# A hybrid recurrence and MoE layer on one core: the last eight gate projections move ahead of the gated-delta steps

## The chip, the cores and the metric

The kernel runs on 1 core of one Trainium2 chip. Times are device microseconds (us) of one execution, as the chip measures them. The profile and its trace come from one more execution, whose own time is given beside its span.

## What is computed

One layer over 256 latent tokens with a 256-token context, width 1024, all in f32: a projection, two bidirectional recurrences (gated delta and RWKV-7) that run first over the context and then over the latent tokens, a gated merge, and a mixture of 32 experts.

```
  u  = RMSNorm(h) * (1 + scale1) + shift1
  p  = u @ W_in                                  # also the columns of both gates gA, gB
  yA = GatedDeltaNet(p[A cols])                  # 4 + 4 chunks of 64, both directions
  yB = RWKV7(p[B cols])                          # bidirectional, column-major grid order
  h += gate1 * W_out( sig(p[gA]) * yA @ W_oA + sig(p[gB]) * yB @ W_oB )
  h += gate2 * HierMoE( RMSNorm(h) * (1 + scale2) + shift2 )

def step(s, inp):                                # one chunk of the gated delta rule
    v_new = u_c - w_c @ s
    o_c = qd_c @ s + qk_c @ v_new
    s = s * ge_c + kd_c.T @ v_new
```

The modulation rows (gate1, shift2, scale2, gate2) are products of silu(c) with the columns 2048 to 6143 of ada_w. They and the gates read only u and c, so neither depends on a recurrence.

## The kernel before, in words

Python writes the operations in program order and a scheduler orders each engine's instructions by their dependencies, by the buffers that they take in rings, and by priorities. The order of the middle of the program is a string, NB['go']; each letter calls one part (L1605), and some letters carry a priority (NB['hi']; G and r have none):

```
for x in NB["go"]:
    with hi(x):
        parts[x]()
TG, gm = t[2], n["G"]
...
k.rwkv_g()
...
k.gate_cols(range(max(gm, NB["g1"]), 16), ("pj", "ch", "ch"))
```

- **G** (filler, L1590) is one gate tile through gate_cols (L1052): a projection of 128 columns (proj, L350: 8 matmuls 128x256, which the trace shows as 16 records `pj<-u,w`, with two weight loads of 256 KB), a tanh on ACT, and a store to gscr. After each odd tile ada_rest (L253) makes one of eight modulation products: 8 matmuls 32x512, 16 records `ada<-w,silc`, with eight loads of 256 KB. Behind the last tile of each half ada_rows stores the sums.
- **r** is one of four latent RWKV-7 steps (rwkv_step; names rps, akps, ups, yps, sps). **R** is the same for the context. K, g, k, i, I, J, q, Q, V prepare the gated delta rule.
- gdn_step (L970) is one of eight gated-delta steps (0 to 3 context, 4 to 7 latent): it loads keys gkc and values gvc from scratch memory, transposes them (gkt, gvt), then gks (keys by state gS), gr on DVE, gup (by the triangular inverse TG), guu on ACT, gsp (state update), gS on DVE; a latent step also has gop, 16 pairs of small matmuls that give its output yo. gdn_post (L1039) ends the branch: a square on ACT, gon, Ln and Exp on ACT with a table load between them, two products on DVE.
- rwkv_post normalizes the RWKV-7 output (mean, then gate<-bg, yc). merge_b (L1083) multiplies it by w_o (`pab<-yc,w`), merge_a (L1093) does so for the gated-delta output (`pab<-post,w`), out_rows (L1100) multiplies by w_out into acc, and moe_quad (L1277) handles groups of four experts, whose weights wgu and wd (per expert 1024 x 512 and 256 x 1024 in f32) are streamed from HBM on SP's queue into six and seven slots.

Weight tiles of proj, ada_rest, merge and out_rows share a ring of 10 buffers of 256 KB (wraw, L340, pool "w"). From L1623 on a second pool "w2" of 12 buffers takes its place until the merge of the gated-delta branch. PSUM is divided in tags (L97): pj is one buffer of 512 columns, gc two, ch two. Gate tiles in filler use pj alone (NB['gt']). rwkv_g (L433) makes projection tile 30 with the tags EARLY (pj, gc, gc) and stands in program order behind the loop. gdn_step's gks, gup, gsp and gop use gc; gkt and gvt use pp.

Of the kernel before, what the change touches and what calls it, by code (L numbers as in the profile page):

```python
# [99 lines left out]
class K:  # L100
    def __init__(self, ctx, tc, A, dbg=None):
        self.nw = NB["w"]
        self.ctx, self.tc, self.nc, self.A, self.dbg = ctx, tc, tc.nc, A, dbg or {}
# [55 lines left out]
    def e(self, name, *dims, rows=P):  # L159
        return self.t(self.pe, name, *dims, tag="e", bufs=NB["e"], w=520, rows=rows)  # L160

    def rt(self, name, *dims):
        return self.t(self.prt, name, *dims, tag="rt", bufs=NB["rt"], w=520)

# [65 lines left out]
    def ada_first(self, hf, pool):  # L230
        ps = self.psum(NB["at"][0], name="ada0")[:, 0:512]

        for k in range(KD):
            w = self.t(pool, "aw", 2, 512, bufs=16)
            self.nc.sync.dma_start(w, self.A["ada_w"][k * P:(k + 1) * P, 0:2 * D]
                                   .rearrange("p (v c) -> p v c", v=2)[:, :, hf * 512:(hf + 1) * 512])
            for v in range(2):
                g = 2 * (k % 2) + v
                self.mm(ps[32 * g:32 * g + 32, :], self.sc[:, k, :], w[:, v, :], start=k < 2, stop=k > 5)
        a = self.e("a0", 512)  # L240
        self.nc.vector.tensor_copy(a, ps)
        pt = self.psum(NB["at"][1], name="adat")
        for j in range(4):
            self.lastada = self.mm(pt[:, j * 64:(j + 1) * 64], a[:, j * P:(j + 1) * P], self.cst("fold")).ins
        pv = pt[:, 0:256].rearrange("p (j v r) -> p v r j", j=4, v=2)[:, :, 0:2]
        m = self.mod[:, :, :, 4 * hf:4 * hf + 4]
        par = lambda n, v: self.parw(n).rearrange("p (v k) -> p v k", v=v)[:, :, 4 * hf:4 * hf + 4]
        for r in range(2):
            self.tt(m[:, :, r], pv[:, :, r], par("adab", 2), ALU.add)
            self.stt(m[:, 1, r], m[:, 1, r], 1.0, par("g1", 1)[:, 0], ALU.add, ALU.mult)  # L250


    def ada_rest(self, i, tags):  # L253
# [5 lines left out]
        if q == 0:  # L259
            self.copy(self.arow[b], ps, NB["aa"])  # L260
        else:
# [1158 lines left out]
EP0 = ((("wgu", 1), ("wd", 0)), (("wgu", 2), ("wd", 1)))  # L1420
EP1 = (("wgu", 3), ("wgu", 4), ("wd", 2))
PRE = (("wgu", 0), ("wgu", 1), ("wgu", 2), ("wd", 0), ("wgu", 3), ("wd", 1), ("wd", 2), ("wd", 3))
NB = {'st': 2, 'ys': 'PP', 'yc': [1, 1], 'hn': 'VAVA', 'im': 'AAPP', 'e': 7, 'rt': 13, 'w': 10, 'e1': 4, 'o2': 2, 'kvr': 2, 'cv': 'PVVPPVPPPVVV', 'g1': 3, 'g2': 0, 'imt': 1, 'gi': 0, 'hi': {'gp': 2000, 'R': 2000, 'i': 2000, 'gs': 2000, 'I': 2000, 'J': 2000, 'p11': 200, 'j0': 1500, 'g': 400, 'V': -400, 'rw': 2000}, 'zf': 1, 'g0': 1, 'pe': 0, 'vr': 'vr', 'jt': 'pp', 'go': 'KGGgGGRRGRRikIVGQqJrrrrG', 'rX': 1, 'rbk': 2, 'ixt': 1, 'vh': 2, 'bk': 4, 'ar': 3, 'gm': 7, 'fp': [[28, 'pj'], [29, 'gc'], [20, 'gc'], [21, 'ch'], [22, 'ch']], 'at': ['pp', 'sc'], 'pf': {'ma': 2, 'oo': 0.5}, 'pm': 8, 'aa': 1, 'gr': 0, 'gu': ['pj', 'gc', 'gc'], 'gq': 2, 'gk': 2, 'w2': 12, 'ip': [0, 0, 4], 'gt': ['pj']}


def layout(inp):
# [303 lines left out]
```

## Time and profile before

| | |
|---|---|
| median of 3 runs | 893.25 us (891.11 to 895.0) |
| the profiled execution | 896.1 us, its span 894.3 us |
| TensorE (PE) busy | 799.8 us, 89% of the span |
| VectorE (DVE), ScalarE (ACT), GpSimd (POOL) busy | 383.6, 229.2, 193.2 us |
| mean granted TensorE clock | 0.921 of full speed |
| HBM read, written | 189.64 MB, 19.94 MB |

Busy time is the time in which an engine executes. A granted clock of 1.00 is 2.4 GHz, of 0.5 is 1.2 GHz; a stretch between them had some time at each. "[0.63 <-DMA gkc<-kscr]" behind an instruction says that its engine was idle for 0.63 us before it and that the DMA into gkc ended the wait.

### The profile page before, as it was taken

The numbers are of one execution on the slowest core, as the hardware profiler recorded it, in microseconds if no ns is written. First come the engines' busy times: TensorE is split into PE (matmuls) and PEld (weight loads), VectorE is DVE, ScalarE is ACT, GpSimd is POOL, SyncE is SP. The second block draws the span as 40 slices with busy tenths as digits, with TensorE's granted clock in tenths as the row PEclk, the third lists the DMA queues.
The fourth block names the chain that finished last, engine by engine and source line by source line (L and its number), as shares of the span: only waits on it lengthen the run. The fifth ranks groups of instructions, "written<-read, shape, count | busy, mean of one in ns | idle before, by whom it ended". The sixth has DMA issues, their size and how long they took to land. (4 is left out here: it accounts for less than half of the span.)

```text
span 894.3 us, 15035 instructions
## 1 busy us (share of the span) xinstructions
PE 799.8 (89%) x6073; PEld 472.5 (53%) x6073; DVE 383.6 (43%) x799; ACT 229.2 (26%) x430; POOL 193.2 (22%) x279
## 2 busy tenths in 40 slices
PE   6999999898569999999899999999978996897785
PEld 1444567444246665767688776768444442332231
DVE  1322878999479446963235312133252210111012
ACT  0413465342363313344312231040030000000001
POOL 1012444336332626734211010000120000000000
PEclk9999999799668999997879988899999998998998
DMA  9722556323517762564641686666965999999993
GB/s 353 301 94 71 167 172 212 116 95 127 175 60 228 232 203 79 153 196 130 198 147 53 238 325 194 219 200 225 405 287 235 428 425 425 423 429 423 427 413 138
DMA packets 88359, 210.58 MB, mean 235 GB/s; under 512 B 7752, under 2 KB 37200, under 8 KB 80864
## 3 DMA queue, kind: packets, MB, share of 16 engines
q1 hardware_dynamic: 85248, 205.87, 62.9%
q10 hardware_dynamic: 3040, 3.74, 1.2%
q8 instruction: 48, 0.79, 0.4%
q14 instruction: 23, 0.19, 0.1%
HBM read 189.64 MB, written 19.94 MB: 234 GB/s over the span
## 5 line engine op out<-in xcount | busy, mean ns | idle before, releaser
L106 PE MATMUL pj<-u,w 128*128 128x256 f32 (+1 forms) x768 | 253.9, 483 | 2.5 <-ACT cxp L122 1.6
L106 PEld LDWEIGHTS pj<-u,w 128*128 128x128 f32 x768 | 146.2, 197 | 96.5 <-issue 75.6
L106 PE MATMUL gup<-wgu,xs 128*32 128x512 f32 x512 | 78.3, 678 | 22.1 <-DMA wgu<-in_wgu_dram 22.0
L106 PEld LDWEIGHTS gup<-wgu,xs 128*32 128x32 f32 x512 | 20.3, 122 | 76.1 <-issue 41.6
L112 DVE TENSOR_TENSOR msg<-msg,gup 128x256 f32<-128x256 f32 x8 | 3.4, 421 | 119.7 <-ACT msg L122 119.7
L112 POOL TENSOR_TENSOR rl<-rl,mhalf 128x1 f32<-128x1 f32 x2 | 1.1, 550 | 224.8 <-DVE rl L116 224.8
L112 DVE TENSOR_TENSOR itm<-ixt,imt 128x31 f32<-128x31 f32 (+22 forms) x89 | 40.1, 450 | 6.1 <-POOL ixt L546 4.1
L112 DVE TENSOR_TENSOR ixt<-ixt,itm 128x31 f32<-128x31 f32 (+22 forms) x89 | 41.6, 467 | 2.2
L106 PE MATMUL dnp<-wd,mhT 128*32 128x512 f32 x256 | 38.6, 598 | 4.1 <-DVE mhT L1326 4.1
L122 ACT ACT_TABLE_LOAD x24 | 30.8, 1283 | 22.4 <-PE ssq L106 10.4
L112 POOL TENSOR_TENSOR cacc<-cacc,cm 128x512 f32<-128x512 f32 (+1 forms) x24 | 26.5, 1106 | 43.1 <-ACT cm L122 31.6
L106 PEld LDWEIGHTS xsp<-oh,h 128*128 128x128 f32 x256 | 31.8, 199 | 6.2 <-issue 6.2
L106 PE MATMUL xsp<-oh,h 128*128 128x128 f32 x256 | 33.2, 283 | 0.0
L122 ACT ACTIVATE msg<-gup 128x256 f32<-128x256 f32 x8 | 3.1, 384 | 111.3 <-PE gup L106 111.3
L106 PE MATMUL acc<-my,ohT 128*128 128x512 f32 x64 | 29.7, 596 | 0.0
L106 PE MATMUL acc<-w,m 128*128 128x512 f32 x64 | 28.4, 594 | 0.6 <-DMA w<-in_w_out_dram 0.6
L112 POOL TENSOR_TENSOR gS<-gS,sdec 128x1024 f32<-128x1024 f32 x6 | 11.5, 1915 | 76.4 <-PE gop L106 45.2
L122 ACT ACTIVATE xs<-xsp 128x512 f32<-128x512 f32 x8 | 4.8, 597 | 90.4 <-PE xsp L106 90.4
L112 POOL TENSOR_TENSOR h<-xres,rowscale 128x512 f32<-128x512 f32 x4 | 5.1, 1270 | 105.1 <-DVE xres L112 105.1
L112 POOL TENSOR_TENSOR shs<-xp 128x512 f32<-128x512 f32 (+1 forms) x15 | 15.1, 1005 | 48.6 <-ACT xp L122 48.6
L106 PE MATMUL akps<-rA,rX 64*64 64x64 f32 x512 | 21.7, 241 | 2.8 <-ACT rtm L122 1.4
L106 PE MATMUL ada<-aw,silc 128*32 128x512 f32 x64 | 16.7, 716 | 8.2 <-DMA aw<-in_ada_w_dram 8.1
(371 smaller groups left out, 1305.3 us busy)
## 6 DMA issues: line engine op xcount, KB each, us to landing
wgu<-in_wgu_dram SPq DMA_DIRECT2D x28, 2048.0 KB
wd<-in_wd_dram SPq DMA_DIRECT2D x27, 1024.0 KB
w<-in_w_in_dram SPq DMA_DIRECT2D x96, 256.0 KB
w<-in_ada_w_dram SPq DMA_DIRECT2D x64, 256.0 KB
aw<-in_ada_w_dram SPq DMA_DIRECT2D x16, 512.0 KB
rX<-rscr SPq DMA_DIRECT2D x8, 768.0 KB
wgu<-in_wgu_dram SPq DMA_DIRECT2D x20, 256.0 KB
rscr<-bk SPq DMA_DIRECT2D x8, 512.0 KB
```

The lines of the kernel that those rows point to most:

```text
L106: return self.nc.tensor.matmul(out, lhsT, rhs, start=start, stop=stop)
L112: (eng or self.nc.vector).tensor_tensor(out=out, in0=a, in1=b, op=op)
L122: return self.nc.scalar.activation(out=out, in_=in_, func=func, **kw)
```

## The change

Eight more G stand at the end of the string, so the loop makes all sixteen gate tiles (tile 0 is made earlier, elsewhere), and with them the modulation products 4 to 7 and the second ada_rows. The call of gate_cols at L1625 then has an empty range. Nothing is added or removed: 8 projections, 8 tanh, 8 stores, 4 modulation products, and 48 loads (12.6 MB) are issued at another place in program order. They use the ring of pool "w" and the PSUM tag pj in place of "w2" and pj, ch, ch.

```
-'go': 'KGGgGGRRGRRikIVGQqJrrrrG'
+'go': 'KGGgGGRRGRRikIVGQqJrrrrGGGGGGGGG'
```

What the scheduler makes of it on PE is shown at two places; the rows are instructions in issue order, with the buffers' numbers only where a name needs one. The first is the start of the gated-delta chain, in the kernel before:

```order
L106 MATMUL rps<-ruv,rak 64x64 x8
L106 MATMUL rps<-sbd_1518,rA 64x128
L109 MATMUL gkt<-cs,gkc 128x128 x4
L106 MATMUL kqp<-gq,gk 64x64 x8
L106 MATMUL rps<-sbd_1518,rA 64x128 x4
L106 MATMUL gup<-gr_4602,TG 64x128 x8
L106 MATMUL rps<-sbd_1518,rA 64x128 x3
L106 MATMUL akps<-rA,rX 64x64 x18
L106 MATMUL gsp<-guu,gkd 128x128 x8
L106 MATMUL ups<-rr_3908,iT 64x64 x13
L106 MATMUL gks<-gS,gkc 64x128
L106 MATMUL ups<-rr_3908,iT 64x64 x3
```

The first gup and gsp (gr_4602 is that of step 0) stand among the matmuls of a latent RWKV-7 step. After the change, PE has these rows right behind the last `yps` of the last latent step:

```order
L106 MATMUL pj<-u,w 128x256 x8
L106 MATMUL mean<-yo,cs 128x512 x2
L106 MATMUL pj<-u,w 128x256 x8
L106 MATMUL mean<-ysq,cs 128x512 x2
L106 MATMUL ada<-w,silc 32x512 x8
L106 MATMUL pj<-u,w 128x256
L106 MATMUL gup<-gr_4602,TG 64x128 x8
L106 MATMUL pj<-u,w 128x256 x7
L106 MATMUL gsp<-guu,gkd 128x128 x8
L106 MATMUL gks<-gS,gkc 64x128 x8
L106 MATMUL gvt<-cs,gvc 128x128 x4
L106 MATMUL gate<-bg,g_4475 128x256 x4
```

The first two pj are gate tiles 14 and 15, the third is projection 30 of rwkv_g; gup of step 0 has moved behind them, and with it all eight gated-delta steps. The second place is the end of the chain, the last gop of step 7 and what follows it. Before:

```order
L106 MATMUL gop<-gqc,gS 128x64
L106 MATMUL gop<-gdq,guu 128x64
L106 MATMUL pab<-yc,w 128x256 x12
L106 MATMUL gon<-yo,cs 128x512
L1132 MATMUL shp<-cs,sh 128x8
L106 MATMUL pab<-yc,w 128x256 x16
L106 MATMUL pab<-post,w 128x256 x3
```

And after:

```order
L106 MATMUL gop<-gqc,gS 128x64
L106 MATMUL gop<-gdq,guu 128x64
L106 MATMUL gon<-yo,cs 128x512
L1132 MATMUL shp<-cs,sh 128x8
L1132 MATMUL shp<-wr,shc 128x36 x8
L106 MATMUL pab<-post,w 128x256 x16
L106 MATMUL acc_5327<-w,m 128x512
```

The matmuls `pab<-yc,w` of merge_b no longer stand between gop, gon and `pab<-post,w`: after the change all 32 lie between gate<-bg and gsp, gks of the steps 1 to 3, and the 8 matmuls of shp are the only ones behind gon. Of steps 4 to 7 PE has only their own matmuls.

## Rows read from the trace of the kernel before

**Rows 1.** Busy time by stage: start:end, length, each engine, PEclk, DMA share, GB/s.

```profile
388.00:500.00 112.00, 105.62 (x1619) 84.64 (x1620) 42.59 (x90) 36.02 (x81) 26.03 (x28) 0.86 0.42 133
500.00:608.00 108.00, 107.03 (x575) 77.95 (x575) 26.15 (x56) 25.16 (x43) 4.29 (x3) 0.89 0.71 242
608.00:655.00 47.00, 46.40 (x163) 28.59 (x162) 12.35 (x26) 2.53 (x6) 2.54 (x2) 1.00 0.80 299
655.00:685.00 30.00, 22.15 (x156) 14.29 (x154) 14.27 (x58) 6.69 (x14) 6.09 (x6) 0.89 0.67 281
685.00:876.00 191.00, 159.10 (x979) 64.72 (x980) 28.00 (x64) 6.54 (x14) 0.00 (x0) 0.94 1.01 421
```

**Rows 2.** The end of the RWKV-7 recurrence on PE: start us, us, what, [idle before].

```profile
499.73 0.28 PE L106 MATMUL yps<-rbk,ruv 128*64 128x64 f32 x2
499.94 1.09 PE L106 MATMUL gup<-gr,TG 64*64 64x128 f32 x16
501.66 0.63 PE L109 MATMUL gkt<-cs,gkc 128*128 128x128 f32 x4 [0.63 <-DMA gkc<-kscr]
```

**Rows 3.** The first expert group on PE, the queue behind it, and the end of out_rows.

```profile
651.05 3.60 PE L106 MATMUL acc<-w,m 128*128 128x512 f32 x8
...
677.45 7.07 PE L106 MATMUL gup<-wgu,xs 128*32 128x512 f32 x64
...
684.53 2.13 SPq L337 DMA_DIRECT2D wgu<-in_wgu_dram  x4
```

**Rows 4.** PE's largest wait from 388 to 500 us: total, times, longest.

```profile
PE kqp L106 <- DMA gq<-qscr: 2.1, 2, 1.4
```

**Rows 5.** Shorter stretches, in the columns of rows 1.

```profile
417.00:434.00 17.00, 17.00 (x260) 13.27 (x259) 3.67 (x8) 6.41 (x12) 4.85 (x4) 0.54 0.33 94
...
460.00:500.00 40.00, 39.05 (x629) 32.20 (x629) 19.63 (x44) 9.76 (x25) 7.66 (x4) 1.00 0.17 48
...
572.50:580.00 7.50, 7.50 (x28) 5.81 (x28) 1.18 (x3) 0.63 (x1) 0.00 (x0) 0.54 0.58 213
```

**Rows 6.** One projection, and one modulation product, on PE.

```profile
372.48 3.72 PE L106 MATMUL pj<-u,w 128*128 128x256 f32 x16 [1.61 <-ACT cxp L122]
...
394.99 1.92 PE L106 MATMUL ada<-w,silc 128*32 128x512 f32 x16
```

**Rows 7.** One step's state update and the next key product, PE and DVE.

```profile
494.23 1.71 PE L106 MATMUL gsp<-guu,gkd 64*128 64x128 f32 x16
...
495.49 1.28 DVE L112 TENSOR_TENSOR gS<-gS,gsp 128x512 f32<-128x512 f32 x2 [2.46 <-PE gsp L106]
```

**Rows 8.** The activation behind the triangular product, ACT, and the key load, SP's queue.

```profile
501.13 0.60 ACT L122 ACTIVATE guu<-gup 128x512 f32<-128x512 f32 x1 [0.57 <-PE gup L106]
...
498.83 0.32 SPq L976 DMA_DIRECT2D gkc<-kscr  x1
```

**Rows 9.** The output matmuls of step 6, first and last pair of 16, on PE.

```profile
569.29 0.43 PE L106 MATMUL gop<-gdq,guu 64*128 64x64 f32 x2
...
575.65 0.69 PE L106 MATMUL gop<-gdq,guu 64*128 64x64 f32 x2
```

**Rows 10.** The last gdn_post and what follows it: PE, ACT and DVE.

```profile
587.13 1.08 PE L106 MATMUL gon<-yo,cs 128*128 128x512 f32 x2
...
599.83 1.02 PE L106 MATMUL gon<-yo,cs 128*128 128x512 f32 x2
...
612.70 1.87 PE L106 MATMUL shp<-wr,shc 128*128 128x36 f32 x16
...
591.58 0.63 ACT L122 ACTIVATE yo<-yo 128x512 f32<-128x512 f32 x1
...
600.89 0.69 ACT L122 ACTIVATE yo<-gon,eps 128x512 f32<-128x512 f32 x1 [5.54 <-PE gon L106]
601.60 1.28 ACT L122 ACT_TABLE_LOAD   x1
...
604.49 0.68 DVE L112 TENSOR_TENSOR post<-yo,post 128x512 f32<-128x512 f32 x1
```

More of the change, by code (lines that the diff above doesn't have):

```diff
@@ L1422 @@
 PRE = (("wgu", 0), ("wgu", 1), ("wgu", 2), ("wd", 0), ("wgu", 3), ("wd", 1), ("wd", 2), ("wd", 3))
-NB = {'st': 2, 'ys': 'PP', 'yc': [1, 1], 'hn': 'VAVA', 'im': 'AAPP', 'e': 7, 'rt': 13, 'w': 10, 'e1': 4, 'o2': 2, 'kvr': 2, 'cv': 'PVVPPVPPPVVV', 'g1': 3, 'g2': 0, 'imt': 1, 'gi': 0, 'hi': {'gp': 2000, 'R': 2000, 'i': 2000, 'gs': 2000, 'I': 2000, 'J': 2000, 'p11': 200, 'j0': 1500, 'g': 400, 'V': -400, 'rw': 2000}, 'zf': 1, 'g0': 1, 'pe': 0, 'vr': 'vr', 'jt': 'pp', 'go': 'KGGgGGRRGRRikIVGQqJrrrrG', 'rX': 1, 'rbk': 2, 'ixt': 1, 'vh': 2, 'bk': 4, 'ar': 3, 'gm': 7, 'fp': [[28, 'pj'], [29, 'gc'], [20, 'gc'], [21, 'ch'], [22, 'ch']], 'at': ['pp', 'sc'], 'pf': {'ma': 2, 'oo': 0.5}, 'pm': 8, 'aa': 1, 'gr': 0, 'gu': ['pj', 'gc', 'gc'], 'gq': 2, 'gk': 2, 'w2': 12, 'ip': [0, 0, 4], 'gt': ['pj']}
+NB = {'st': 2, 'ys': 'PP', 'yc': [1, 1], 'hn': 'VAVA', 'im': 'AAPP', 'e': 7, 'rt': 13, 'w': 10, 'e1': 4, 'o2': 2, 'kvr': 2, 'cv': 'PVVPPVPPPVVV', 'g1': 3, 'g2': 0, 'imt': 1, 'gi': 0, 'hi': {'gp': 2000, 'R': 2000, 'i': 2000, 'gs': 2000, 'I': 2000, 'J': 2000, 'p11': 200, 'j0': 1500, 'g': 400, 'V': -400, 'rw': 2000}, 'zf': 1, 'g0': 1, 'pe': 0, 'vr': 'vr', 'jt': 'pp', 'go': 'KGGgGGRRGRRikIVGQqJrrrrGGGGGGGGG', 'rX': 1, 'rbk': 2, 'ixt': 1, 'vh': 2, 'bk': 4, 'ar': 3, 'gm': 7, 'fp': [[28, 'pj'], [29, 'gc'], [20, 'gc'], [21, 'ch'], [22, 'ch']], 'at': ['pp', 'sc'], 'pf': {'ma': 2, 'oo': 0.5}, 'pm': 8, 'aa': 1, 'gr': 0, 'gu': ['pj', 'gc', 'gc'], 'gq': 2, 'gk': 2, 'w2': 12, 'ip': [0, 0, 4], 'gt': ['pj']}
 def layout(inp):
```

## The prediction

> **What bounds the kernel now.** I read the busy time by stage first [rows 1], then the PE timeline at the stages' borders [rows 2, 3], and last the waits and shorter stretches inside them [rows 4, 5]. From 388 us (latent RWKV-7 steps, gated-delta preparation) to 655 us (out_rows) TensorE sets the time: it is busy 105.62 of 112 us, then 107.03 of 108, then 46.40 of 47. What it loses there is idle time, 6.4 us before 500 and 1.6 after (0.97 + 0.60), and clock: 112 x (1 - 0.86) = 15.7 us and 108 x (1 - 0.89) = 11.9 us. From 685 to 876 us the DMA engines set the time (share 1.01, 421 GB/s), while the expert weights stream.
>
> Between these lies the coupling. The next weights wait in SP's queue at 684.53 us, right when the first expert group's gup ends (677.45 + 7.07 = 684.52) [rows 3]: all weight slots are full, and the stream restarts only when TensorE has read a group. So the first group's end plus some 210 us is the end of the kernel (894.3 - 684.5). From acc's end, 654.65, to that group lies routing of fixed length. A delay of out_rows is therefore a delay of the end, one to one; the expert stream doesn't hide it, and being early gains one to one too.
>
> **What is moved.** Eight projections at 3.72 us and four modulation products at 1.92 [rows 6]: 29.8 + 7.7 = 37.4 us of PE work, with 48 loads (12.6 MB). They leave a place where TensorE was 99% busy. None disappears, so over 388 to 655 us the PE work at equal clock is unchanged, and the result is the sum of what idle time and clock change by, in three places: the front (before the last yps of the RWKV-7 recurrence, ends at 500.0 [rows 2]), the gated-delta chain, and its end.
>
> **The front.** The order puts six of the eight projections and three of the products there, and takes steps 0 to 3 of the gated-delta rule and projection 30 out. The loads cost nothing there: 12.6 MB in 112 us is 112 GB/s beside 133 [rows 1], well below the 421 that the engines reach. As filler the projections can cover the waits: 6.4 us in all, the largest with 2.1 for gq [rows 4]. I take half, 3 us, since a filler has no priority and fewer filler instructions are ready when its one PSUM buffer pj is waiting for ACT. Clock: the loss sits in a few stretches, as 417 to 434 us at 0.54 with TensorE 100% busy [rows 5], which follow idle time. If less idle time precedes them, fewer come. I take 4 of the 15.7. Front: **-7** (between 0 and -22, everything recovered).
>
> **The chain.** In program order, rwkv_g's projection and the gated-delta steps, which share the PSUM tag gc with it, now stand behind all gate tiles, and rwkv_g takes its weights from the same ten buffers. So gup of step 0 comes after the last gate tile (the first place shown) instead of inside the latent recurrence, and the eight steps run with merge_b's 32 matmuls as their only filler, which are used up in steps 1 to 3. What hid each step's waits before was the gate tiles; now TensorE sees them:
> - After gsp the state is added on DVE. gsp ends at 495.94, gS at 496.77 [rows 7]: 0.8 us until gks may start. The order has gsp right ahead of gks twice, and once with gkt's 0.63 us between (0.2 left): 1.9 us.
> - After gup, guu: 501.03 to 501.73 [rows 2, 8], 0.7 us with nothing between in two steps, 0.1 in two others: 1.6 us.
> - gkc of a later step is issued behind gks and landed 2.83 us later before (498.83 [rows 8] to 501.66, where TensorE waited 0.63 for it [rows 2]). The steps now follow each other faster in the first four, and 1 MB pieces of expert weights stand in the same queue: 1 us in each of three steps, 3 us.
> - Projection 30 stands behind the last gate tile's loads and w_o's in SP's queue: 3.25 to 4.75 MB ahead of it, at 421 GB/s 8 to 11 us, and 13 us of PE work after the recurrence to cover it, of which the wait for landing takes a part: 3 us (0 to 6).
>
> **The end of the chain.** Before, merge_b's matmuls lay between the last gop, gon and `pab<-post,w` (the second place shown). Now two things are bare. gup of step 7 stands behind the first gon, so its guu stands on ACT behind the table load, Ln, table load, Exp of gdn_post: from 588.21 (gon's end) to 592.21 (Exp's end) [rows 10], 4.0 us, plus guu 0.6 [rows 8], less gup's 1.09 and one gop at 0.36: 3.2 us. And behind the last gop come the add to yo (0.5), the square (0.7), gon, then Ln, table load, Exp, two DVE products: 600.85 to 605.17 [rows 10], 4.3 us. Cover is only shp, 0.2 + 1.87 [rows 10]. Left: 0.5 + 0.7 + 4.3 - 2.1 = 3.4 us.
>
> Sum of idle time: 1.9 + 1.6 + 3 + 3 + 3.2 + 3.4 = 16.1, less the 1.6 of before that falls away: **+14.5** (bounds 7, if loads and projection 30 are hidden and half of the rest, and 22, if loads cost double).
>
> **The clock in the chain.** The first gop pairs of a step take 0.36 us each, the last 0.62 [rows 9]: TensorE falls to 1.2 GHz (0.54 from 572.5 to 580 us [rows 5]) although it is busy. Four such falls make most of the 11.9 us. The gop stay; between them, where dense projections stood, now come idle gaps. I take half as much again, **+6** (0: gaps as short as these don't matter, as in 460 to 500 us, where sparse 64-wide products ran with 1 us idle at 1.00 [rows 5]; 20: everything from step 3 to the end, some 50 us, at 0.6).
>
> A rule that weighs against the change: the Trainium skill, TensorE: Matmul & The Clock Gate, section "What's actually happening", says that throttled is the default state and that activity releases it. By that rule steps 4 to 7 without filler would spend most of their time at 1.2 GHz, and the term would be its upper bound, 20. The trace agrees in part: 655 to 685 us with 7.9 us idle had 0.89 [rows 1], but 417 to 434 without any idle had 0.54.
>
> **The sum.** -7 + 14.5 + 6 = +13.5, on the profiled 896.1: 910. The profiled execution lies 2.9 us above the median 893.25, so against the median 907; I say **908**, since the bounds reach farther above the sum (22 and 20) than below it. No change means within 0.5%, 4.5 us, about what a measurement of this kernel can tell: 889 to 898.
>
> **Rivals.**
> - *The front gives everything back.* The projections fill all waits and the clock stays up there: -22 in place of -7. With +20.5 behind, that is 893 - 1.5, 892: the same. For it: the moved work is twice the size of idle time and falls together. Against: 417 to 434 fell with no idle in it, so filling can't remove that one (17 x 0.46 = 8 us).
> - *Faster, by the clock of the gop.* If the four falls from 552 on come of the mixture of dense projections and small gop, which now are apart, 11.9 us come back where I add 6, and the front returns 10: -10 + 14.5 - 11.9 = -7, 886. It decides for faster where the falls vanish and the front gives 7 or more. Against: gop were at 1.2 GHz in a stretch that was theirs alone.
> - *The delay is hidden.* If the expert stream had time to spare, out_rows could be 14 us late and the end stay: 893. Against: the queue waits at 684.53 for TensorE, not the reverse.
> - *The chain at half clock.* By the rule above, and with ten buffers stalling the queue for the gate loads: -3 + 20 + 18 = +35, 928. For it: in steps 4 to 7 TensorE waits some 10 us of 50.
>
> **How the numbers follow.** My sum 0.57; much slower 0.13; the front gives everything back 0.11; hidden 0.05; faster 0.14. My sum's own range is 899 to 920. Range 886 to 922: below lies half of the faster case (0.08), above most of the half clock (0.09). Faster by over 0.5%: 0.14; within 0.5%: 0.16, the front's case and the hidden one; slower: 0.70.
>
> **What would show it.** Right: in the profile after, gup of step 0 behind the last yps; the stretch up to that yps as long as before or a few us shorter; 14 us or more of PE idle time from there to acc's end, with releasers gkc, guu, gS, gon or post; shp directly ahead of `pab<-post,w`; the first expert group's gup some 13 us later and the rest of the kernel, 210 us, unchanged. Wrong: the front shorter by 15 us or more; chain idle time below 7; granted clock in the chain above 0.95; or the stretch from the first expert group to the end shorter than 205 us.

## The result, and the profile after

The changed kernel took a median of 922.22 us over 4 runs (919.93 to 926.98), the kernel before 894.12 over 4 runs beside them: a ratio of 1.0326, 95% interval 1.028 to 1.0373, or 28 us slower. The forecast had the direction and the places right; its 908 was 14 us too low, and its range ended at 922.0. The profiled execution of the changed kernel is the slowest of the four (926.98, span 925.2), 4.8 us above their median.

The stages first, in the columns of rows 1, cut at the last yps of the RWKV-7 recurrence (497.3), the first gop (571.4), the end of the last gop (632), the first `pab<-post,w` (640.7), the end of acc and the first expert group:

```profile
388.00:497.30 109.30, 103.86 (x1543) 80.95 (x1543) 33.82 (x66) 32.74 (x69) 20.05 (x27) 0.91 0.63 202
497.30:571.40 74.10, 62.52 (x402) 46.91 (x401) 26.52 (x55) 14.90 (x30) 8.25 (x5) 0.91 0.72 247
571.40:632.00 60.60, 56.43 (x270) 44.68 (x270) 11.88 (x28) 10.00 (x20) 3.82 (x2) 0.59 0.17 57
632.00:640.70 8.70, 5.73 (x20) 4.14 (x20) 2.57 (x5) 4.51 (x5) 0.00 (x0) 0.50 0.81 274
640.70:684.60 43.90, 43.90 (x138) 26.47 (x139) 11.21 (x24) 2.53 (x6) 2.54 (x2) 0.96 0.62 215
685.00:715.00 30.00, 22.30 (x156) 14.44 (x154) 14.26 (x58) 6.54 (x14) 6.08 (x6) 0.89 0.68 281
715.00:907.00 192.00, 160.18 (x979) 64.75 (x980) 28.03 (x64) 6.68 (x14) 0.00 (x0) 0.92 1.01 420
```

Beside [rows 1]: the front is a little better (idle 5.4 us, clock 0.91), the expert stream is the same, and everything is lost between 497 and 641 us. There TensorE is idle for 11.6 us, then 4.2, then 3.0. And in the third row the profile calls it 93% busy at a granted clock of 0.59, in the fourth 0.50: most of steps 4 to 7 and the whole of the end ran at 1.2 GHz.

The same in the PE timeline, and SP's queue for the last row (compare [rows 2, 3, 9, 10]):

```profile
497.04 0.28 PE L106 MATMUL yps<-rbk,ruv 128*64 128x64 f32 x2
517.12 1.22 PE L106 MATMUL pj<-u,w 128*128 128x256 f32 x2 [5.87 <-DMA w<-in_w_in_dram]
518.27 1.97 PE L106 MATMUL gup<-gr,TG 64*64 64x128 f32 x16
...
575.03 0.43 PE L106 MATMUL gop<-gqc,gS 128*128 128x64 f32 x2
575.39 0.54 PE L106 MATMUL gop<-gdq,guu 64*128 64x64 f32 x2
575.86 0.69 PE L106 MATMUL gop<-gqc,gS 128*128 128x64 f32 x2
...
604.06 1.71 PE L106 MATMUL gsp<-guu,gkd 64*128 64x128 f32 x16 [0.75 <-ACT guu L122]
606.49 0.69 PE L106 MATMUL gop<-gdq,guu 64*128 64x64 f32 x2
...
620.80 0.43 PE L106 MATMUL gop<-gqc,gS 128*128 128x64 f32 x2
...
631.27 0.69 PE L106 MATMUL gop<-gdq,guu 64*128 64x64 f32 x2
633.13 2.08 PE L106 MATMUL gon<-yo,cs 128*128 128x512 f32 x2 [1.18 <-ACT yo L122]
637.25 3.63 PE L106 MATMUL shp<-wr,shc 128*128 128x36 f32 x16 [1.84 <-DVE shc L1134]
640.68 8.71 PE L106 MATMUL pab<-post,w 128*128 128x256 f32 x32
...
707.60 7.07 PE L106 MATMUL gup<-wgu,xs 128*32 128x512 f32 x64
...
714.68 2.10 SPq L337 DMA_DIRECT2D wgu<-in_wgu_dram  x4
```

Projection 30 waits 5.87 us for its weights, and gup of step 0 stands behind its first matmul. Inside step 4's gop, with no idle time before it in that group, the pace drops from 0.36 to 0.62 us. From there on the clock is 0.50 from 575.8 to 602.8, from 606.4 to 620.0 and from 623.4 to 641.5 us; it comes back twice, for 3.6 and 3.4 us behind the gup of steps 6 and 7, and is lost again within the gop that follow. A gon takes 2.08 us where it took 1.02 [rows 10], shp 3.63 in place of 1.87. The first expert group starts 30.15 us later than before; the queue restarts at its end, and from there to the end are 210.5 us (925.2 - 714.7), where 209.8 stood before. So the whole loss lies ahead of the experts.

PE's waits in the changed kernel from 497 to 685 us (total, times, longest), the largest of 13 rows:

```profile
PE pj L106 <- DMA w<-in_w_in_dram: 5.9, 1, 5.9
PE gkt L109 <- DMA gkc<-kscr: 2.6, 3, 2.0
PE shp L106 <- DVE shc L1134: 1.8, 1, 1.8
PE gop L106 <- ACT guu L122: 1.7, 1, 1.7
PE gsp L106 <- ACT guu L122: 1.5, 2, 0.8
PE gup L106 <- DVE gr L119: 1.2, 2, 0.6
PE gon L106 <- ACT yo L122: 1.2, 1, 1.2
```

What the clock took is read from equal matmuls. The gop groups of the changed kernel (busy us, mean ns of one):

```profile
L106 PE MATMUL gop<-gdq,guu 64*128 64x64 f32 x64 | 20.3, 415 | 1.7 <-ACT guu L122 1.7
L106 PE MATMUL gop<-gqc,gS 128*128 128x64 f32 x64 | 20.0, 411 | 0.6 <-DVE gS L112 0.6
```

and of the kernel before:

```profile
L106 PE MATMUL gop<-gdq,guu 64*128 64x64 f32 x64 | 15.5, 326 | 0.3 <-ACT guu L122 0.3
L106 PE MATMUL gop<-gqc,gS 128*128 128x64 f32 x64 | 14.9, 318 | 0.0
```

The same 128 records (four steps of 16 matmuls, two records each) take 9.9 us more. By the same groups from 388 to 690 us, gsp, gks, gup, gkt with gvt, gon and shp take 1.9, 1.7, 2.2, 1.1, 2.1 and 1.7 us more, 20.6 with gop; the dense ones (pj, ada, pab, gate) take 6.3 less. With 16.1 us more of idle time (17.1 more behind the last yps, 1.0 less before it) this is 30.4, against the 30.15 measured at the first expert group.

### The profile page after: what moved, and what is told of

It is laid out like the page before. It is cut to its first block, busy times and chain, and to the rows that moved or that the text cites. A ratio compares the mean times of both kernels' runs of the same rounds, so it can differ in the third digit from the quotient of the medians.

```text
span 925.2 us, 15057 instructions
## 1 busy us (share of the span) xinstructions
PE 817.4 (88%) x6073; PEld 487.5 (53%) x6073; DVE 387.7 (42%) x799; ACT 229.1 (25%) x430; POOL 193.8 (21%) x279
## 5 line engine op out<-in xcount | busy, mean ns | idle before, releaser
L112 DVE TENSOR_TENSOR ixt<-ixt,itm 128x31 f32<-128x31 f32 (+22 forms) x89 | 39.4, 442 | 2.2
L116 DVE TENSOR_SCALAR shtm<-pj,omu 128x256 f32<-128x256 f32 x25 | 12.0, 479 | 30.8 <-ACT xp L122 30.8
L106 PE MATMUL ada<-aw,silc 128*32 128x512 f32 x64 | 16.6, 717 | 8.5 <-DMA aw<-in_ada_w_dram 8.4
L106 PE MATMUL akps<-rA,rX 64*64 64x64 f32 x512 | 19.8, 233 | 3.6 <-ACT rtm L122 1.4
```

The lines of the kernel that those rows point to most:

```text
L106: return self.nc.tensor.matmul(out, lhsT, rhs, start=start, stop=stop)
L112: (eng or self.nc.vector).tensor_tensor(out=out, in0=a, in1=b, op=op)
L116: (eng or self.nc.vector).tensor_scalar(out=out, in0=a, scalar1=s1, scalar2=s2, op0=op0, **kw)
```

## The experiments

Theory A at the start: the loss comes from the order. The steps were held back behind projection 30 and the gate tiles, and without dense matmuls beside their gop they fall to 1.2 GHz. Rivals put it on the buffers that the moved tiles use, on the idle gaps, or on the gop themselves. Ratios are to the kernel before, timed beside each set of experiments: 894.88 us for e1 to e4, 895.01 for e5 to e8, 895.25 for e9 to e11.

**e1: projection 30 ahead of the moved tiles** (all eight still moved; "w" calls rwkv_g)

```
-'go': '...JrrrrGGGGGGGGG'        k.rwkv_g() behind the loop
+'go': '...JrrrrGwGGGGGGGG'       "w": k.rwkv_g
```

> The changed kernel, with projection 30 (rwkv_g) moved in program order ahead of the eight extra gate tiles. Theory A (the cost comes from the order: the gated-delta steps were held back behind projection 30 and the gate tiles, and steps 4 to 7 then ran without dense matmuls beside the gop): gate tiles and steps interleave again, the mean granted clock from the last yps to the end of out_rows is 0.88 or more, idle TensorE time there under 4 us, time 888 to 898. Rival B (the cost comes with the ten-buffer ring and the single PSUM buffer that the moved tiles use, wherever they stand): 910 or more.

888.45 us, ratio to the kernel before 0.9942 (0.9906 to 0.9978): 34 us off the changed kernel, and 0.6% below the kernel before, by an interval that ends below 1. Its stages, cut at the last yps, the last gop, 600 us and the end of acc:

```profile
388.00:521.00 133.00, 128.51 (x1789) 102.05 (x1792) 46.37 (x98) 41.12 (x94) 28.88 (x30) 0.94 0.49 159
521.00:584.40 63.40, 62.36 (x364) 44.65 (x363) 18.64 (x40) 15.20 (x23) 1.91 (x1) 0.92 0.76 264
584.40:600.00 15.60, 14.58 (x57) 11.60 (x57) 5.52 (x12) 4.51 (x5) 0.00 (x0) 0.89 0.72 235
600.00:643.10 43.10, 43.10 (x150) 26.20 (x149) 11.23 (x24) 2.53 (x6) 2.54 (x2) 1.00 0.86 320
```

As theory A has it: 2.1 us of idle time behind the last yps, clock 0.89 and more. The tiles use the same ring and PSUM buffer as in the changed kernel, so rival B falls. With projection 30 ahead, the moved tiles come with a gain of some 6 us; since no run has projection 30 ahead and no tile moved, what each of the two is worth stays open.

**e2: projection 30 in the PSUM tag pj alone** (its place unchanged, so the steps no longer wait for it)

```
-        self.shift_cols(self.proj(30, False, self.EARLY), 14, (None, g))
+        self.shift_cols(self.proj(30, False, ("pj",)), 14, (None, g))
```

> The changed kernel, with projection 30 in the PSUM tag pj alone, so that it stays behind the gate tiles but no longer shares a ring with the gated-delta steps. Theory A: the steps run up into the latent RWKV-7 recurrence, all gate tiles 10 to 15 become their filler, time 882 to 897, clock from 388 us to the end of out_rows 0.88 or more. Rival C (gop matmuls lower the clock wherever they stand, and by as much): clock near 0.6 over the gop's some 45 us, time 905 or more.

902.05 us, ratio 1.0063 (1.0036 to 1.0091): between both. The stages:

```profile
500.00:550.00 50.00, 50.00 (x416) 37.34 (x414) 10.04 (x22) 6.96 (x18) 3.82 (x2) 0.76 0.34 108
550.00:577.00 27.00, 27.00 (x137) 18.13 (x137) 7.31 (x17) 7.29 (x8) 0.00 (x0) 0.88 0.94 353
577.00:663.00 86.00, 78.91 (x294) 53.17 (x295) 23.91 (x50) 12.38 (x19) 3.15 (x3) 0.96 0.72 247
```

The shared PSUM ring did hold the steps back: now gop begin at 503 us, while yps still run until 550. But there the latent recurrence's 64-wide matmuls are their company, and the clock is 0.76 with TensorE 100% busy; the dense tiles come later, and 7.1 us of idle time at the end. Over 388 to 663 us the clock is 0.89, as theory A asked, but the time is 5 us over its range; the gop groups take 33.3 us, more than in the kernel before (30.4) and less than in the changed one (40.3), so rival C's "by as much" falls. Being early is not enough.

**e3: dense matmuls added beside the gop of the changed kernel**

```
                 pv = ps[:, 0:256].rearrange("p (h n) -> p h n", h=NH)
+                pd = self.psum("pj", name="dum")
                 for h in range(NH):
+                    self.mm(pd[:, 0:L], self.cst("ones"), u[:, 0:2, :])
```

> The changed kernel, with one 128x256 matmul added for each gop pair of 2 (32 in all, about 15 us by the 0.465 us of one in a projection at 2.4 GHz, results unused). Theory A (1.2 GHz in steps 4 to 7 comes of the lack of dense matmuls between the gop): the clock of these steps rises from 0.59 to 0.8 or more, and the gain of some 20 us pays for the added work: 910 to 923. Rival D (the clock falls for the idle gaps, or for the gop as such): the clock stays near 0.6, added work costs 15 to 30 us: 937 to 952.

926.34 us, ratio 1.0371 (1.0309 to 1.0434): 4 us above the changed kernel, although the added matmuls take 22.8 us in the trace. Steps 4 to 7 (first to last gop), and the gop groups:

```profile
566.40:625.10 58.70, 54.71 (x320) 43.98 (x318) 10.66 (x25) 10.00 (x20) 3.82 (x2) 0.84 0.19 59
```

```profile
L106 PE MATMUL gop<-gdq,guu 64*128 64x64 f32 x64 | 16.1, 338 | 0.0
L106 PE MATMUL gop<-gqc,gS 128*128 128x64 f32 x64 | 14.4, 312 | 0.0
```

With 24 of the 32 useless matmuls inside it (some 17 us), the stretch is 1.9 us shorter than the changed kernel's 60.6. Its idle time is 4.0 us against 4.2, so the gaps are the same; the clock rises from 0.59 to 0.84, and the gop are back at 30.5 us. Rival D falls on both counts: gaps and gop are the same as in the changed kernel, and with dense matmuls among them the clock isn't held down. It still falls in places, in the gop of steps 5 and 7. Which property of the added matmuls counts, their width or that they wait for nothing, is not told apart. The total is 3 us over theory A's range.

**e4: the moved tiles left out of the kernel before** (gate_cols from tile 8 on)

```
-            ps = self.proj(31 + 8 * br + j, False, tags)
+            ps = self.proj(31 + 8 * br + j, False, tags) if i < 8 else None
...
+            if i >= 8:
+                self.nc.gpsimd.memset(t, 0.0)
...
-            if i % 2:
+            if i % 2 and i < 8:
```

> The kernel before, with gate tiles 8 to 15 and modulation products 4 to 7 left out (zeros are stored in their place): 37.4 us of TensorE work and 12.6 MB of loads less. Theory A (these tiles hold TensorE's clock and cover the waits while the steps run): most of the saving is lost, clock under 0.75 from the last yps to the last gon, time 872 to 892. Rival E (the work is simply worth its time): 850 to 862.

867.31 us, ratio 0.9666 (0.9612 to 0.972), between both theories' ranges: 27.6 of the 37.4 us are saved. From the last yps to the last gop, and to the last gon and the rest of the bare end:

```profile
501.00:579.30 78.30, 74.36 (x387) 57.47 (x386) 22.28 (x49) 16.88 (x29) 3.83 (x2) 0.77 0.51 174
579.30:590.00 10.70, 8.06 (x26) 5.96 (x26) 2.77 (x6) 4.51 (x5) 0.00 (x0) 0.50 0.72 245
```

The clock falls as theory A says (0.73 over both rows, where 0.89 stood before), the idle time is 6.6 us, and about a quarter of the 37.4 us is lost. Less than I expected; its order has merge_b among the gop of steps 5 to 7, which may be why, but no run tells that apart.

**e5: four tiles moved in place of eight**

```
-'go': '...JrrrrGGGGGGGGG'
+'go': '...JrrrrGGGGG'
```

> Four extra gate tiles behind the latent steps in place of eight, the other four where they were; projection 30 stays behind the moved ones. In its order gup of step 0 stands inside the last latent step, but steps 5 to 7 again have no gate tile between their gop. Theory A (the time lies in the clock of the steps without dense matmuls, and in the bare end of the chain): granted clock under 0.7 over steps 5 to 7, time 903 to 917. Rival F (only the last gate tiles cost, by the late weights of projection 30 and the late start of the chain): 890 to 900.

904.2 us, ratio 1.0116 (1.0076 to 1.0156). As theory A has it: gop from 545 us, no idle time until then, and a clock of 0.68 over 545 to 607 us, 0.57 over steps 5 to 7 alone (565 to 607). The time lies above rival F's range: the loss doesn't come only with the last tiles.

**e6: the weights of projection 30 loaded early** ("w" issues the two loads, its matmuls stay in rwkv_g)

```
-'go': '...JrrrrGGGGGGGGG'
+'go': '...JrrrrGGGGGGwGGG'
```

> The changed kernel, with the two weight loads of projection 30 issued three gate tiles earlier, its matmuls where they were. In its order step 0 starts inside the last latent step, since projection 30 is ready sooner; steps 4 to 7 are as bare of dense matmuls as in the changed kernel. Theory A: the wait of 5.9 us is gone and a few us of idle time with it, the clock of steps 4 to 7 stays near 0.6, time 909 to 918. Rival F (late weights and the late start are most of the cost): 903 or less.

905.02 us, ratio 1.0127 (1.0075 to 1.0178): 17 us off the changed kernel, twice what I expected from the wait, 4 us below theory A's range and 2 above rival F's. From the last yps to the first gop, to the last, and the bare end:

```profile
502.60:551.20 48.60, 48.60 (x330) 35.17 (x330) 21.05 (x46) 11.56 (x22) 5.74 (x3) 1.00 0.84 298
551.20:607.00 55.80, 52.12 (x272) 41.20 (x270) 11.75 (x27) 10.01 (x20) 3.83 (x2) 0.64 0.33 105
607.00:615.50 8.50, 5.70 (x20) 4.08 (x20) 2.57 (x5) 4.51 (x5) 0.00 (x0) 0.50 0.84 284
```

All of the 11.6 us of idle time ahead of the first gop is gone, not only the 5.9 for the weights, and the clock there is 1.00 in place of 0.91. Once step 0 starts inside the recurrence, gate tiles, mean, gate and merge_b cover the waits of steps 0 to 3. Steps 4 to 7 and the end are as they were: 0.64 and 0.50. So the loss has two parts: the start, 17 of the 28 us, which this edit takes away, and the clock of steps 4 to 7 with the end, which stay. Against e1, where the same tiles move and the clock is up, what stays is 16.6 us; against the kernel before it is 10.

**e7: as e1, with four tiles**

```
-'go': '...JrrrrGwGGGGGGGG'
+'go': '...JrrrrGwGGGG'
```

> As the run with projection 30 ahead, but with four extra gate tiles in place of eight. Its order has merge_b's matmuls beside the gop of step 7 and none left behind the last gon. Theory A: clock in the gop stretch 0.85 or more, the end of the chain bare as in the changed kernel (some 3 to 5 us of idle time), time 888 to 897. Rival G (the gain of projection 30 ahead grows with the tiles moved): halfway between the kernel before and the run with eight, 889 to 893, with no idle time at the end.

894.41 us, ratio 1.001 (0.9969 to 1.0051): in theory A's range and 1.4 us past rival G's, which the interval, 3.7 us to either side, can't tell apart. The clock is 0.88 over the gop stretch (509.3 to 592.6 us), as theory A asked, but the end is less bare than it said: behind the last gop TensorE waits 2.1 us, of them 1.8 for post, which e1 doesn't have.

**e8: as e1, projection 30 one tile earlier**

```
-'go': '...JrrrrGwGGGGGGGG'
+'go': '...JrrrrwGGGGGGGGG'
```

> As the run with projection 30 ahead, one gate tile earlier still. Theory A (once the chain has dense work beside it, nothing more is to be had from the order of this tile): 884 to 894, the same as that run within its interval. Rival H (each tile that projection 30 is moved past frees the chain further): 883 or less.

899.51 us, ratio 1.0059 (1.0026 to 1.0092). Neither: 11 us slower than e1. The chain ends early (last gop at 569.56), and three gate tiles and two modulation products are left over behind it, with waits of their own. PE's waits from 480 to 690 us have these, which e1 doesn't have:

```profile
PE pab L106 <- DVE post L119: 4.3, 1, 4.3
PE pj L106 <- DVE arow L112: 2.9, 1, 2.9
PE pab L106 <- DVE arow L112: 0.9, 1, 0.9
```

Here the filler outlasted the chain, and the place of one tile decided it.

**e9: merge_b held back for steps 4 to 7 of the changed kernel** (no work added)

```
+                    if i > 3:
+                        with k.tc.issue_after(k.lastgup):
+                            k.merge_b(y, tbs, range(2 * i - 8, 2 * i - 6))
```

> The changed kernel, with merge_b's 32 matmuls held back so that 8 stand behind gup of each of the steps 4 to 7, instead of all in steps 1 to 3. No work is added. Theory A (steps 4 to 7 are slow for want of dense matmuls beside the gop, and the start for its bare waits, each by itself): the clock of steps 4 to 7 rises from 0.59 to 0.7 or more and gives back 6 to 14 us, the waits of steps 1 to 3 lose their cover and cost 3 to 8 more: 912 to 920. Rival D (dense matmuls help only in the number of e3, some 15 us or more): clock below 0.65, time 922 to 930.

921.19 us, ratio 1.0317 (1.0256 to 1.0378): no change, 1 us over theory A's range. The stretches are first from the last yps to the first gop, then to the last:

```profile
490.10:560.50 70.40, 55.10 (x352) 40.74 (x352) 22.65 (x49) 14.87 (x30) 8.26 (x5) 0.85 0.62 215
560.50:623.00 62.50, 60.59 (x318) 48.61 (x318) 14.21 (x34) 10.02 (x20) 3.82 (x2) 0.72 0.27 83
```

Both halves are there: steps 4 to 7 take in 24 matmuls more and are 2 us longer (clock 0.72, gop 34.6 us in place of 40.3), and give back 11 us, since those matmuls take 12.8; meanwhile the first stretch holds 15.3 us of idle time instead of 11.6, its clock falls from 0.91 to 0.85, and it is only 3.7 us shorter for the work that left it. Some 15 us of dense work can't do both.

**e10: e6 and e9 together**

> The weights of projection 30 early, as in the run with these loads moved, and merge_b's matmuls held back for steps 4 to 7. Theory A (the two parts add): what the holding back gave or took on the changed kernel it gives or takes on the run with early weights too, within 5 us, so 893 to 905. Rival I (with an earlier start the same gaps are hidden anyway): same as the run with early weights alone, 902 to 908, with the clock of steps 4 to 7 still near 0.64.

901.0 us, ratio 1.0073 (1.0039 to 1.0108): 4 us less than e6, where e9 took 1 us from the changed kernel. They add within the 5 us that I had put down, with intervals as wide as the difference. The time is 1 us below rival I's range and can't decide; the clock, 0.72 over 545 to 608 us, speaks against it.

**e11: as e1, the gop of steps 4 and 5 without priority**

```
         if lat:
+          with self.tc.high_priority(-2000) if s < 6 else ExitStack():
```

> As the run with projection 30 ahead, with the gop of steps 4 and 5 without the priority of the other matmuls of a step, so that they mix with the gate tiles. In its order merge_b is used up before the last gon. Theory A: the clock of the gop stretch rises from 0.92 to 0.95 or more (2 to 4 us), the bare end costs 3 to 4: 886 to 893, not better than that run. Rival H (mixing is worth more than the end): 883 or less.

890.38 us, ratio 0.995 (0.9923 to 0.9978): as good as e1, not better. Idle time from 509.5 to 592.7 us is none, but the clock there is 0.92 as in e1, not the 0.95 that I expected, and the bare end is back with 0.50 over 8 us.

## Why the prediction was right and wrong

**Coupling: right.** The queue restarts at the end of the first expert group, and the 30.15 us of delay there are nearly all of the 30.9 of the span. The rival that the stream hides it falls.

**Front, -7: right in sum, by terms that missed either way.** It takes in six projections and three products (28.1 us by [rows 6]) and gives away some 24 us, at full clock too, of steps 0 to 3 and projection 30, and ends 2.7 us earlier (497.3 against 500.0 [rows 2]): about -7. But idle time fell by 1.0 us where I had 3, and the wait for gq, which the filler was to cover, grew from 2.1 to 3.6 [rows 4]. The clock rose from 0.86 to 0.91, 5.9 us by my own measure (15.7 less 109.3 x 0.09) where I had 4. My reason for that, less idle time ahead of the falls, is not shown: the idle time hardly changed.

**Idle time in the chain, +14.5: right in size, shifted inside.** 18.7 us against 1.6, so +17.1. The weights of projection 30 took 5.9 where I had 3, at the bound; gr with 1.2 was not on the list; step 7's guu took 1.7 in place of 3.2. gkc (2.6), guu (1.5), gS (1.5) and the end (1.2 + 1.8) came as forecast. What I had not seen is that these belong together: e6 shows that late weights made the start bare as a whole, 17 us with the clock.

**The clock, +6: wrong, this is the step that failed.** With the front at -7 and idle time at +17, 20 us are left of the 30.15, where I took +6 and had 20 as the far end. Steps 4 to 7 ran at 0.59 and the end at 0.50. I had let a row decide that has no gop in it: 460 to 500 us at 1.00 with 64-wide products [rows 5]. The row that had them was beside it: 572.5 to 580 us at 0.54 with TensorE 100% busy, the last gop of step 6 and the projection behind them. Before, such a fall came in each of the four gop groups, from some 514, 545, 572 and 593 us (the rival's "from 552 on" is a slip), dense matmuls (pj, ada, pab) followed, and the clock was back after 3 to 7 us. Without them the falls last 27, 14 and 18 us. e3 shows by adding dense matmuls that they shorten them. My reason for the term, idle gaps, is not borne out: in e3 the gaps are the same and the clock is not, and the fall of 27 us starts within a group of gop without a gap. (A shorter one, from 562 to 568 us, did follow a wait of 1.96 for gkc.) The row at 1.00 still sets a limit to this: without a single pj, ada or pab, the small matmuls of the recurrence and of steps 0 to 3 kept 2.4 GHz for 40 us. What in the gop lets the clock fall, no run tells.

The sentence of the Trainium skill that I had weighed (TensorE: Matmul & The Clock Gate, "What's actually happening": throttled is the default, and activity releases it) gave 20 for this term. The trace agrees in the clock, 0.59 over 60.6 us, but not if activity is read as busy time: from 606.4 to 620 us TensorE was 100% busy at 0.50, and two stretches at 93% had 0.59 and, in e3, 0.84. The rival built on it, the chain at half clock, to which I gave 0.13, is what happened in its main part: it added 20 for the clock and 18 for idle time to a front of -3, where 20, 17 and -7 were measured.

**The rivals on the fast side fall.** The front gave 7, not 22; the gop's falls did not vanish but spread.

## What to carry to other kernels

Before dense work is moved ahead, look at what it stood beside: if small matmuls in a dependent chain stay behind, the dense ones may have been both the cover for their waits and, as beside the gop here, what brought TensorE back to 2.4 GHz, and a busy share near 100% shows neither. Look also at what is queued behind the moved work in the same rings: one projection behind eight tiles held eight steps back, and putting it ahead turned a loss of 3.3% into a gain of 0.6%. One tile further ahead it was a loss of 0.6% again (e8): a filler has to last as long as the chain, so its amount and its place are tried together.

## What was not expected of the hardware

TensorE was at 1.2 GHz for 49 of 60.6 us while the profile had it 93% busy, 36 of the 56 busy us with the gop, 64-column f32 matmuls that each follow a weight load (PEld 44.7 us of 60.6). Adding some 17 us of 128x256 matmuls to that stretch made it 1.9 us shorter. And leaving 37.4 us of dense work out of the kernel before saved 27.6.
